# RWKV-7 in the second block's mixer: three pairs of heads through one chain of 384-column tiles

## The chip, the cores and the metric

One core of a Trainium2 chip. The metric is the device time of one execution in microseconds (us), lower is better. The kernel before takes 3003.26 us, the median of 3 runs (3002.71 to 3004.96).

## The reference, cut to what matters

The program is two transformer blocks in fp32 on 256 tokens of width 1024. The second block has two layers, each a feed-forward net, a mixer and another feed-forward net. The change is in that mixer, in its RWKV-7 part alone. It has 6 heads of 64.

```
p_a, p_b, p_c = _split(h @ w_in[l], (A_IN, B_IN, C_IN))     # layer 1 has p_mv too
r, k, v, w_lo, a_lo, g_lo = _split(shift_lerp(p_a, rwkv_mu[l]), A_SLAB)
o_a = rwkv7_mixer(r, k, v, ...)
o_b = dsa_mixer(...)          # 6 heads, 64 of up to 256 keys by an index score
o_c = retention_mixer(...)    # 4 heads
x = x + concatenate([o_a, o_b, o_c]) @ w_out[l]

# rwkv7_mixer, per head and token, S is 64x64:
sa = S @ a_t
S  = S * w_t + outer(sa, b_t) + outer(v_t, k_t)
y  = S @ r_t
y  = head_layernorm(y) * ln_w + ln_b + sum(r * k * r_k) * v
o  = y * g
```

In layer 1, v is mixed with layer 0's v first (`vfirst`).

## The kernel before, in words

`mix2` (L975) is the mixer of one layer. Its columns of `w_in` come in blocks of 128: `blk(i)` (L993) gives block i as a 128x256 product in PSUM (tag `pj`, two banks). `chunk` brings the weights of two blocks with one 1 MB DMA on SP's queue (L130), splits them into `wh` on ACT (L151) and `wl` on DVE (L152), and `mm3` (L158 to L160) makes three fp32r matmuls of every fp32 product: 24 a block, called projections here. They are the work that can fill TensorE while other work waits for other engines.

The order of the blocks in layer 0: 0 and 1 are the low-rank inputs `la` and `iwmv`; 2 to 4 are r, k, v of the first pair of heads, 5 to 7 of the second; 8 to 13 are the latent keys `ct` and the index keys and queries of the sparse attention, then its scores (L1062) and top-k (L1072, L1073); 14 to 16 are its queries `qd`, and six attention heads follow (L1092 to L1119); 17 to 19 are the third pair's r, k, v; 20 to 25 and `w_in_v` feed the retention (L1168 to L1183). Then comes `out_proj`, which needs all parts.

`rwkv` (L1187) does one pair of heads, a 128x256 tile (two heads on the partitions, 256 tokens in 4 chunks of 64). It has three parts:

- **Preparation** (L1237 to L1287), a chain of small operations on ACT, DVE, POOL and TensorE, from the square of k (L1269) to `da` and `db` (L1283).
- **Doubling** (L1301 to L1311): the inverse of a triangular 64x64 matrix per chunk and head, in 5 levels. A level is a masked copy `nm` on POOL (L1303), the product `tN·nm` (16 records on TensorE, L1209), `z` copied out by ACT (L1305), two more products, and the new `tN` and `tT` on DVE (L1308, L1310).
- **Steps** (L1324 to L1350): 4 chunks one after another. In each, `U` is copied out by ACT (L1330), the state `sn` is made on DVE (L1342) from a product and from `sd`, the old state scaled on POOL (L1341), and the output goes to `yT` (L1348). Layer norm and gate end the pair (L1352 to L1359).

Instructions are written in program order. A framework puts each on its engine's queue, by that order and by when it takes its inputs to be ready, and every engine runs its queue in a fixed order. So the place of a call decides which other work lies between its instructions. PSUM has 8 banks, by tags: `mm` 3, `pj` 2, `pr` 1, `ax` 2.

Of the kernel before, what the change touches and what calls it, by code (L numbers as in the profile page):

```python
# [73 lines left out]
class Net:  # L74
# [900 lines left out]
    def mix2(s, l, upd):  # L975
# [4 lines left out]
        with ExitStack() as cx:  # L980
# [24 lines left out]
            def lerp(p, mu, out):  # L1005
                nmu = s.small.tile([P, 1], F32, name="nmu", tag="nmu")
                V.tensor_scalar(nmu, mu, -1.0, 1.0, op0=OP.mult, op1=OP.add)
                t = k.tile([P, S + 1], F32, name="lt", tag="lt", bufs=1)
                nc.gpsimd.memset(t[:, 0:1], 0.0)
                V.tensor_tensor(t[:, 1:], p, r, OP.mult)  # L1010
                d = one("ld")
                nc.scalar.activation(d, t[:, 1:], AF.Copy, scale=nmu)
                V.scalar_tensor_tensor(out, t[:, :S], mu, d, op0=OP.mult, op1=OP.add)
                return out
# [15 lines left out]
            def rwkv(pr, b0):  # L1030
                x = [lerp(blk(b0 + i), s.col(f"mu{l}", 3 * i + pr), one("rkv", N_RKV)) for i in range(3)]
# [6 lines left out]
            V.tensor_tensor(ct, blk(8), r, OP.mult)  # L1038
            ike, iko = s.zeroed(k, 1, S, "ik")
            p = blk(9)  # L1040
# [3 lines left out]
            for b in range(4):  # L1044
                V.tensor_tensor(iq[:, b], blk(10 + b), r, OP.mult)
# [33 lines left out]
            for b in range(3):  # L1079
                V.tensor_tensor(qd[:, b], blk(14 + b), r, OP.mult)  # L1080
# [41 lines left out]

            rwkv(2, 17)
# [63 lines left out]
    def rwkv(s, l, pr, x, la, iwmv, w2, v2, cn, w, oh, ol):  # L1187
# [5 lines left out]
        rows = [slice(64 * h, 64 * h + 64) for h in range(2)]  # L1193

        def four(m):
            return m[:, None, :].to_broadcast([P, 4, 64])

        def nat(v):
            return v.rearrange("p (c t) -> p c t", c=4)

        def t1(name, bufs=1):
            return w.tile([P, S], F32, name=name, tag=name, bufs=bufs)

        def u(name):
            return nat(w.tile([P, S], F32, name=name, tag="u", bufs=N_SLOT))

        def mul(o, a, b, start=True, stop=True):
            for h, rr in enumerate(rows):
                nc.tensor.matmul(o[rr], a[rr], b[rr], start=start, stop=stop, tile_position=(64 * h, 64 * h))  # L1209

        def prod(a, b):
            p = nat(s.ax(S))
            for c in range(4):
                mul(p[:, c], a[:, c], b[:, c])
            return p

        def turn(name, x):
            p = s.ax(S).rearrange("p (g h t) -> p g h t", g=2, h=2)
            for g in range(2):
                nc.tensor.transpose(p[:, g].rearrange("p h t -> p (h t)"), x[:, 2 * g:2 * g + 2].rearrange("p c t -> p (c t)"), s.ident)  # L1220
            o = u(name)
            for c in range(2):
                for h, rr in enumerate(rows):
                    v, i = o[rr, c:4:2], p[64 * c:64 * c + 64, :, h]
                    nc.scalar.activation(v, i, AF.Copy)
            return o
# [20 lines left out]
        p = s.bank("pr", S)  # L1247
# [15 lines left out]
        dcs = s.small.tile([P, 4], F32, name="dcs", tag="dcs")  # L1263
        nc.gpsimd.tensor_copy(dcs, dd[:, 63:256:64])
# [4 lines left out]
        nc.scalar.activation(sq, kt, AF.Square, scale=s.col(f"k_k{l}", pr))  # L1269
        V.scalar_tensor_tensor(kk, kt, s.col(f"k_k{l}", pr), s.rstd(sq, 1, 2, tag="pr", floor=1e-12),  # L1270
# [3 lines left out]
        V.scalar_tensor_tensor(kt, t, 1.0, kt, op0=OP.add, op1=OP.mult)  # L1274
# [3 lines left out]
        V.scalar_tensor_tensor(t, rt, s.col(f"r_k{l}", pr), kt, op0=OP.mult, op1=OP.mult)  # L1278
        bo = t1("bo", 2)
        V.tensor_tensor(bo, s.bones(t, "pr"), vt, OP.mult)  # L1280
        nc.gpsimd.tensor_tensor(rt, rt, dd, OP.mult)
        da, db, dk, dr = u("da"), u("db"), u("dk"), nat(rt)
        V.scalar_tensor_tensor(da, nat(kk), -1.0, nat(sg), op0=OP.mult, op1=OP.mult)  # L1283
        V.tensor_tensor(db, nat(kk), nat(at), OP.mult)
        lab = u("lab")
        nc.scalar.activation(lab, prod(db, da), AF.Copy)
        nc.gpsimd.tensor_tensor(dk, nat(kt), nat(di), OP.mult)  # L1287
        vs = turn("vs", nat(vt))
        lak = u("lak")
        V.tensor_tensor(lak, prod(dk, da), four(cn("lt")), OP.mult)  # L1290
        X = u("x")
        nc.scalar.activation(X, prod(lak, vs), AF.Copy)
# [19 lines left out]
        w1 = u("w1")
        nc.scalar.activation(w1, prod(as_, tT), AF.Copy)

        mrb = u("mrb")
        V.tensor_tensor(mrb, prod(db, dr), four(cn("le")), OP.mult)
        bs = turn("bs", db)
        mrk = u("mrk")
        V.tensor_tensor(mrk, prod(dk, dr), four(cn("le")), OP.mult)
        ks = turn("ks", dk)  # L1320

        yT = t1("yT")
        st = None
        for c in range(4):  # L1324
            p = s.ax(64)
            mul(p, tT[:, c], X[:, c], stop=(c == 0))
            if c:
                mul(p, w1[:, c], st, start=False)
            U = w.tile([P, 64], F32, name="U", tag="U", bufs=2)
            nc.scalar.activation(U, p, AF.Copy)  # L1330
            if c < 3:
                p = s.ax(64)
                mul(p, ks[:, c], vs[:, c], stop=False)
                mul(p, bs[:, c], U, start=False)
                dc = dcs[:, c:c + 1]
                sn = w.tile([P, 64], F32, name="sn", tag="sn", bufs=3)
                if c == 0:
                    V.tensor_scalar(sn, p, dc, None, op0=OP.mult)
                else:
                    sd = w.tile([P, 64], F32, name="sd", tag="sd", bufs=2)  # L1340
                    nc.gpsimd.tensor_scalar(sd, st, dc, None, op0=OP.mult)  # L1341
                    V.scalar_tensor_tensor(sn, p, dc, sd, op0=OP.mult, op1=OP.add)  # L1342
            yp = s.ax(64)
            mul(yp, vs[:, c], mrk[:, c], stop=False)
            if c:
                mul(yp, st, dr[:, c], start=False, stop=False)
            mul(yp, U, mrb[:, c], start=False)
            V.tensor_copy(yT[:, 64 * c:64 * c + 64], yp)  # L1348
            if c < 3:
                st = sn  # L1350

        V.scalar_tensor_tensor(yT, s.bones(yT), -1.0 / 64, yT, op0=OP.mult, op1=OP.add)  # L1352
        sq = t1("tz1")
        nc.scalar.activation(sq, yT, AF.Square)
        V.scalar_tensor_tensor(yT, yT, s.col(f"ln_w{l}", pr), s.rstd(sq, 64, 2, tag="ax", eps=64e-5),
                               op0=OP.mult, op1=OP.mult)
        V.scalar_tensor_tensor(yT, yT, s.col(f"ln_b{l}", pr), bo, op0=OP.add, op1=OP.add)
        V.tensor_tensor(yT, yT, gt, OP.mult)
        s.split(oh, ol, yT)  # L1359
# [140 lines left out]
def host_w_in(w, mv):  # L1500
# [9 lines left out]
    bl += [P * (3 * i + pr) + r(P) for pr in range(2) for i in range(3)]  # L1510
# [3 lines left out]
    bl += [P * (3 * i + 2) + r(P) for i in range(3)]  # L1514
# [127 lines left out]
```

## Time and profile before

| | before |
|---|---|
| median of 3 runs | 3003.26 us |
| profiled execution | 3003.1 us |
| its span | 3001.1 us (2.0 us lie outside) |
| granted TensorE clock, mean | 0.996 |
| TensorE busy | 2948.9 us (98%) |
| mixer of layer 0, first projection to `out_proj` | 1991.36 to 2202.08, 210.72 us |
| mixer of layer 1 | 2577.10 to 2789.71, 212.61 us |

The page gives busy shares over the whole span, and the trace the start of every instruction. The ends of matmuls are modelled, so a row can be busy while the array waits: the distance from one start to the next says how long something really takes. An fp32 matmul that is not a projection shows as two records.

### The profile page before, as it was taken

What the parts mean: (1) busy time and instruction counts of PE and PEld (TensorE: products, weight loads), DVE (VectorE), ACT (ScalarE), POOL (GpSimd) and SP (SyncE); (2) the same over time, 40 slices, a digit from 0 to 9 for tenths busy, and PEclk for the clock granted to TensorE, in tenths of its full rate; (3) what the DMA queues carried; (4) which work ended last, traced back from release to release, by engine and by line L of the source; (5) the groups of instructions that cost most, each with busy time, mean ns of one, the idle gap of its engine ahead of it and who ended that gap; (6) DMA issues with size and microseconds to landing.
All of it is one profiled execution on the core that took longest, in us unless ns stands there. A gap on an engine that the chain in (4) does not pass through costs nothing.

```text
span 3001.1 us, 53661 instructions
## 1 busy us (share of the span) xinstructions
PE 2948.9 (98%) x21104; PEld 2590.9 (86%) x21104; DVE 2065.5 (69%) x4254; ACT 1520.6 (51%) x3106; POOL 109.7 (4%) x220
## 2 busy tenths in 40 slices
PE   8999999999999999999999999999999999999999
PEld 7888887588888888888877999998799999987998
DVE  5687766787797743335766667786677777866776
ACT  4333354754333442234666556575555655755555
POOL 0000001000000000000000000011100000111000
PEclk9999999999999999999999999999999999999999
DMA  7465422034474422322322555551245555422453
GB/s 281 159 218 194 152 99 85 15 113 169 152 262 165 151 99 92 107 82 99 122 85 99 192 174 193 197 201 54 77 145 198 188 184 190 171 75 69 169 190 127
DMA packets 86988, 434.74 MB, mean 145 GB/s; under 512 B 7888, under 2 KB 19920, under 8 KB 57296
## 3 DMA queue, kind: packets, MB, share of 16 engines
q1 hardware_dynamic: 86736, 431.31, 40.9%
q8 instruction: 166, 2.72, 0.4%
q14 instruction: 86, 0.70, 0.1%
HBM read 430.23 MB, written 1.05 MB: 144 GB/s over the span
## 4 chain that ended last, share of the span: by engine, by line
PE 78%; ACT 2%; DVE 2%; issue 1%; POOL 0%; ACTq 0%; DVEq 0%; POOLq 0%
PE mm L158 10%; PE mm L159 10%; PE mm L160 10%; PE pj L158 8%; PE pj L160 8%; PE pj L159 8%; PE pr L158 3%; PE pr L160 3%; PE pr L159 3%; PE ax L1209 3%; PE ax L562 1%; PE ax L943 1%; PE ax L741 1%; PE ax L220 0%; ACT wh L151 0%
## 5 line engine op out<-in xcount | busy, mean ns | idle before, releaser
L151 ACT ACTIVATE wh<-wr 128x512 fp32r<-128x512 f32 (+1 forms) x1341 | 824.1, 618 | 1055.4 <-PE mm L159 457.7
L152 DVE TENSOR_TENSOR wl<-wr,wh 128x512 fp32r<-128x512 f32 (+1 forms) x1341 | 897.1, 676 | 540.9 <-ACT wh L151 520.2
L158 PE MATMUL mm<-hh,wh 128*128 128x256 f32 (+1 forms) x1592 | 501.3, 315 | 0.1
L159 PE MATMUL mm<-hl,wh 128*128 128x256 f32 (+1 forms) x1592 | 500.8, 315 | 0.4 <-DVE hl L957 0.4
L160 PE MATMUL mm<-hh,wl 128*128 128x256 f32 (+1 forms) x1592 | 500.2, 314 | 0.4 <-DVE wl L152 0.4
L158 PE MATMUL pj<-hh,wh 128*128 128x256 f32 (+1 forms) x1492 | 463.5, 311 | 4.1 <-ACT hh L311 3.1
L160 PE MATMUL pj<-hh,wl 128*128 128x256 f32 (+1 forms) x1492 | 461.8, 310 | 0.2 <-DVE wl L152 0.2
L159 PE MATMUL pj<-hl,wh 128*128 128x256 f32 (+1 forms) x1492 | 459.6, 308 | 0.0
L158 PEld LDWEIGHTS mm<-hh,wh 128*128 128x128 f32 x1592 | 300.4, 189 | 20.9 <-issue 0.3
L159 PEld LDWEIGHTS mm<-hl,wh 128*128 128x128 f32 x1592 | 300.1, 188 | 21.0 <-DVE hl L957 0.8
L160 PEld LDWEIGHTS mm<-hh,wl 128*128 128x128 f32 x1592 | 299.8, 188 | 21.1 <-DVE wl L152 0.8
L254 DVE SCALAR_TENSOR_TENSOR macc<-wm,cv,macc 128x512 f32<-128x512 f32 x448 | 309.1, 744 | 0.6
L158 PEld LDWEIGHTS pj<-hh,wh 128*128 128x128 f32 x1492 | 282.2, 189 | 26.0 <-ACT hh L311 3.9
L160 PEld LDWEIGHTS pj<-hh,wl 128*128 128x128 f32 x1492 | 281.5, 189 | 16.3 <-DVE wl L152 0.4
L159 PEld LDWEIGHTS pj<-hl,wh 128*128 128x128 f32 x1492 | 281.5, 189 | 16.1 <-issue 0.9
L158 PE MATMUL mm<-ah,wh 128*128 128x256 f32 (+1 forms) x721 | 226.3, 314 | 0.0
L160 PE MATMUL mm<-ah,wl 128*128 128x256 f32 (+1 forms) x721 | 226.0, 314 | 0.0
L159 PE MATMUL mm<-al,wh 128*128 128x256 f32 (+1 forms) x721 | 226.0, 313 | 0.0
L158 PE MATMUL pr<-hh,wh 128*128 128x256 f32 (+1 forms) x518 | 166.3, 321 | 0.0
L160 PE MATMUL pr<-hh,wl 128*128 128x256 f32 (+1 forms) x518 | 165.5, 320 | 0.3 <-DVE wl L152 0.3
L159 PE MATMUL pr<-hl,wh 128*128 128x256 f32 (+1 forms) x518 | 165.8, 320 | 0.0
L158 PE MATMUL pj<-ah,wh 128*128 128x256 f32 (+1 forms) x465 | 148.6, 320 | 0.0
(589 smaller groups left out, 5054.3 us busy)
## 6 DMA issues: line engine op xcount, KB each, us to landing
wr<-f_gu SPq DMA_DIRECT2D x85, 1024.0 KB, 4.8
wr<-g_gu SPq DMA_DIRECT2D x84, 1024.0 KB, 4.8
wm<-w_mod SPq DMA_DIRECT2D x64, 1024.0 KB, 4.7
wr<-f_dn SPq DMA_DIRECT2D x64, 704.0 KB, 4.0
wr<-g_dn SPq DMA_DIRECT2D x64, 704.0 KB, 4.0
wr<-w_in_t SPq DMA_DIRECT2D x26, 1024.0 KB, 4.8
ws<-w_mod SPq DMA_DIRECT2D x8, 1024.0 KB, 9.8
wr<-ab_in SPq DMA_DIRECT2D x8, 1024.0 KB, 4.6
```

Source lines behind the costliest of these rows:

```text
L151: s.nc.scalar.activation(h, x, AF.Copy)
L152: s.nc.vector.tensor_tensor(l, x, h.bitcast(F32), OP.subtract)
L158: nc.tensor.matmul(out, lh, rh, start=start, stop=False)
L159: nc.tensor.matmul(out, lh, rl, start=False, stop=False)
L160: nc.tensor.matmul(out, ll, rh, start=False, stop=stop)
L254: nc.vector.scalar_tensor_tensor(acc[u][:, h], w[:, k, h], c, acc[u][:, h], op0=OP.mult, op1=OP.add)
L562: s.nc.tensor.transpose(p[:, b * P:(b + 1) * P], y[:, b * P:(b + 1) * P], s.ident)
L741: nc.tensor.matmul(yp[r], vA[:, k0 + kk, r], pts[e][:, kk], start=(kk == 0), stop=(kk == nk - 1), tile_position=(0, 64 * e))
L943: nc.tensor.matmul(yp[r], v[:, kk, c], pts[e][:, kk], start=(kk == 0), stop=(kk == 3), tile_position=(0, 64 * e))
L1209: nc.tensor.matmul(o[rr], a[rr], b[rr], start=start, stop=stop, tile_position=(64 * h, 64 * h))
```

## The change

- All three pairs' r, k, v come first: the host puts their nine blocks at 2 to 10, and the blocks between move up by 3.
- `rwkv_in` is called three times in a row and does the preparation of one pair. Its results go into tiles that hold all three pairs (`wide`, [128, 2, 3, 128]); its temporaries have one buffer each (so had most before). `vs` is made here, by one transpose per half.
- One call of `rwkv` does doubling and steps for all pairs: half 0 has chunks 0 and 1 of every pair, half 1 has chunks 2 and 3, each a tile of 128x384. The two halves alternate in program order, from level to level. A product is 12 small matmuls and a step handles three pairs at once.
- PSUM tiles of this chain rotate over the tags `ax`, `pr`, `ax`. The preparation uses `mm` and `pr`.
- `sd` on POOL is gone: the old state is added by a matmul with the identity (6 small matmuls in each of two steps), and one multiplication on DVE scales the sum.
- The gate's matmul moves to the end, and its copy `gt` goes; each pair has its layer norm there, ahead of `ct` and the other blocks. The third pair's call behind the heads is gone, and the retention follows the heads directly.

The diff, cut:

```
-N_SLOT = 18
+N_SLOT = 16
-            def rwkv(pr, b0):
-                x = [lerp(blk(b0 + i), ..., one("rkv", N_RKV)) for i in range(3)]
-                s.rwkv(l, pr, x, la, iwmv, w2, v2, cn, k, oh[pr], ol[pr])
-            rwkv(0, 2)
-            rwkv(1, 5)
+            wide = {n: k.tile([P, 2, 3, P], F32, name=n, tag=n) for n in ("rt", "kt", "vt", "da", "db", "vs")}
+            for pr in range(3):
+                for i, n in enumerate(("rt", "kt", "vt")):
+                    lerp(blk(2 + 3 * pr + i), s.col(f"mu{l}", 3 * i + pr), wide[n][:, :, pr])
+                s.rwkv_in(l, pr, la, iwmv, w2, v2, k, wide)
+            s.rwkv(l, la, w2, cn, k, wide, oh, ol)
...
-            rwkv(2, 17)
...
         for m in range(1, 6):
-            nm = u("nm")
-            nc.gpsimd.tensor_tensor(nm, lab, four(lv[:, m]), OP.mult)
-            z = u("z")
-            nc.scalar.activation(z, prod(nm, tN), AF.Copy)
...
+            z = [None, None]
+            for i in both:
+                nm = u("nm")
+                nc.gpsimd.tensor_tensor(nm, lab[i], units(lv[:, m]), OP.mult)
+                z[i] = u("z")
+                nc.scalar.activation(z[i], prod(nm, tN[i]), AF.Copy)
+            for i in both:
+                if m < 5:
+                    n2 = u("tN")
+                    V.tensor_tensor(n2, prod(tT[i], z[i]), tN[i], OP.add)
+                t2 = u("tT")
+                V.tensor_tensor(t2, prod(z[i], tT[i]), tT[i], OP.add)
+                tT[i], tN[i] = t2, n2
...
-                    nc.gpsimd.tensor_scalar(sd, st, dc, None, op0=OP.mult)
-                    V.scalar_tensor_tensor(sn, p, dc, sd, op0=OP.mult, op1=OP.add)
...
+                    if n:
+                        mul(p[:, r], cn("eye"), st[:, r], start=False, stop=False)
+                    mul(p[:, r], bs[i][:, r, c], U[:, r], start=False)
+                sn = state("sn", 2)
+                V.tensor_tensor(sn, p, dcs[:, :, n, None].to_broadcast([P, 3, 64]), OP.mult)
...
+        for pr in range(3):
...
+            p = s.bank("pr", S)
+            nc.tensor.matmul(p, w2[:, 2, pr * P:(pr + 1) * P], la, start=True, stop=True)
+            V.tensor_tensor(y, y, p, OP.mult)
+            s.split(oh[pr], ol[pr], y)
```

What it does to the order on TensorE, at three places of layer 0. A row is line, operation, output and operands, size, and how many in a row. `mul`'s small matmuls are L1209 before and L1289 now; projections are L158 to L160 before and L157 to L159 now. First a level of the doubling, before (the first pair, with work of the preparation of the second between):

```order
L1209 MATMUL ax<-z,tT 64x64 x8
L1209 MATMUL ax<-tT,z 64x64 x8
L1252 MATMUL pr<-la,sm 128x256
L160 MATMUL pj<-hh,wl 128x256
L1209 MATMUL ax<-tN,nm 64x64 x8
L158 MATMUL pj<-hh,wh 128x256
L159 MATMUL pj<-hl,wh 128x256
```

and now:

```order
L1289 MATMUL ax<-tN,nm 64x64 x12
L159 MATMUL pj<-hh,wl 128x256
L157 MATMUL pj<-hh,wh 128x256
L158 MATMUL pj<-hl,wh 128x256
L159 MATMUL pj<-hh,wl 128x256
L157 MATMUL pj<-hh,wh 128x256
L1289 MATMUL pr<-tN,nm 64x64 x12
L1289 MATMUL ax<-z,tT 64x64 x12
L1289 MATMUL ax<-tT,z 64x64 x12
L1289 MATMUL pr<-z,tT 64x64 x12
L1289 MATMUL ax<-tT,z 64x64 x12
L158 MATMUL pj<-hl,wh 128x256
```

A level is now six products of 12, and what stands between a product and the one that needs its result is the other half's product, and a few projections.

Second, the steps. Before (the second pair: `x·tT` and `sn·w` give U, `U·bs` and `vs·ks` the state, the others the output):

```order
L1209 MATMUL ax<-U,bs 64x64 x2
L1209 MATMUL ax<-mrk,vs 64x64 x2
L1209 MATMUL ax<-rkv,sn 64x64 x2
L1209 MATMUL ax<-mrb,U 64x64 x2
L158 MATMUL pj<-hh,wh 128x256
L159 MATMUL pj<-hl,wh 128x256
L160 MATMUL pj<-hh,wl 128x256
L158 MATMUL pj<-hh,wh 128x256
L159 MATMUL pj<-hl,wh 128x256
L1209 MATMUL ax<-x,tT 64x64 x2
```

and now (`con` is the identity):

```order
L1289 MATMUL pr<-x,tT 64x64 x2
L1289 MATMUL pr<-sn,w_20930 64x64 x2
L1289 MATMUL ax<-vs,ks 64x64 x2
L1289 MATMUL ax<-sn,con 64x64 x2
L1289 MATMUL ax<-mrk,vs 64x64 x2
L1289 MATMUL ax<-U,bs 64x64 x2
```

The projections between the steps are gone from here; there are 4 passes instead of 12, each with three times the small matmuls.

Third, the last attention head. Before, the doubling of the third pair and projections stood between its operations:

```order
L1209 MATMUL ax<-z,tT 64x64 x7
L1209 MATMUL ax<-tT,z 64x64
L1119 MATMUL mm<-lat,smd 64x256
L1209 MATMUL ax<-tT,z 64x64 x7
L159 MATMUL pj<-hl,wh 128x256
L160 MATMUL pj<-hh,wl 128x256
L1209 MATMUL ax<-tN,nm 64x64 x8
L1135 MATMUL pj<-z,con 128x256
```

and now:

```order
L159 MATMUL pj<-hh,wl 128x256
L561 MATMUL mm<-ident,pe 128x128 x3
L1117 MATMUL mm<-pt,ck 128x128 x3
L1121 MATMUL mm<-lat,smd 64x256
L1094 MATMUL mm<-qd,smd 128x256
L1103 MATMUL mm<-ct,ql 128x128
L1103 MATMUL mm<-ct,ql 128x256
L561 MATMUL mm<-ident,pe 128x128 x3
L1117 MATMUL mm<-pt,ck 128x128 x3
L1168 MATMUL mm<-qr,kre 128x256
L1121 MATMUL mm<-lat,smd 64x256
L1168 MATMUL mm<-qr,kre 128x128
```

The last head stands nearly alone, and the retention begins while it ends.

## Rows read from the trace of the kernel before

**Rows 1.** The page: busy time by engine over the span.

```profile
PE 2948.9 (98%) x21104; PEld 2590.9 (86%) x21104; DVE 2065.5 (69%) x4254; ACT 1520.6 (51%) x3106; POOL 109.7 (4%) x220
```

**Rows 2.** Windows, both mixers and a dense stretch: length, busy PE, PEld, DVE, ACT, POOL, clock, DMA.

```profile
1991.36:2202.08 210.72, 204.20 (x2313) 172.70 (x2312) 140.61 (x392) 118.52 (x296) 31.92 (x55) 1.00 0.26 89
2577.10:2789.71 212.61, 206.42 (x2320) 173.14 (x2318) 142.98 (x397) 120.33 (x299) 33.60 (x55) 1.00 0.25 88
2300.00:2310.00 10.00, 10.00 (x90) 10.00 (x89) 6.08 (x11) 4.92 (x9) 0.00 (x0) 1.00 0.81 303
```

**Rows 3.** Windows, layer 0's mixer: projections of line L158 alone, then line L1209 alone.

```profile
1991.36:2202.08 210.72, 69.66 (x235) 44.36 (x236) 1.00 0.26 89
...
1991.36:2202.08 210.72, 55.23 (x1248) 44.00 (x1248) 1.00 0.26 89
```

**Rows 4.** Timelines of TensorE, ACT and DVE: one level of the first pair's doubling.

```profile
2038.53 0.68 PE L1209 MATMUL ax<-tN,nm 64*64 64x64 f32 x16
...
2039.36 0.59 PE L972 MATMUL pr<-tmp,con 128*128 128x256 f32 x2
2039.88 0.68 PE L1209 MATMUL ax<-z,tT 64*64 64x64 f32 x16
...
2041.63 0.38 PE L1209 MATMUL ax<-tN,nm 64*64 64x64 f32 x5
...
2039.26 0.38 ACT L1305 ACTIVATE z<-ax 128x256 f32<-128x256 f32 x1 [2.01 <-PE ax L1209]
...
2040.67 0.42 DVE L1308 TENSOR_TENSOR tN<-ax,tN 128x256 f32<-128x256 f32 x1 [0.26 <-PE ax L1209]
```

**Rows 5.** Timelines of TensorE, ACT and DVE: one step of the second pair.

```profile
2092.41 0.28 PE L1209 MATMUL ax<-sn,w 64*64 64x64 f32 x4
2092.53 0.28 PE L1209 MATMUL ax<-vs,ks 64*64 64x64 f32 x4
...
2093.18 0.33 PE L1209 MATMUL ax<-U,bs 64*64 64x64 f32 x4
...
2092.74 0.22 ACT L1330 ACTIVATE U<-ax 128x64 f32<-128x64 f32 x1 [1.60 <-PE ax L1209]
...
2094.76 0.20 ACT L1330 ACTIVATE U<-ax 128x64 f32<-128x64 f32 x1
...
2093.62 0.28 DVE L1342 SCALAR_TENSOR_TENSOR sn<-ax,dcs,sd 128x64 f32<-128x64 f32 x1 [0.53 <-PE ax L1209]
```

**Rows 6.** Timelines of ACT and DVE: preparation begins and ends, layer 0 first pair, layer 1 second.

```profile
2006.62 0.51 ACT L1269 ACTIVATE tmp<-rkv,colt 128x256 f32<-128x256 f32 x1
...
2016.41 0.42 DVE L1283 SCALAR_TENSOR_TENSOR da<-kk,sgw 128x256 f32<-128x256 f32 x1
...
2614.43 0.51 ACT L1269 ACTIVATE tmp<-rkv,colt 128x256 f32<-128x256 f32 x1 [0.96 <-DVE tmp L1240]
...
2632.64 0.41 DVE L1283 SCALAR_TENSOR_TENSOR da<-kk,sgw 128x256 f32<-128x256 f32 x1
```

**Rows 7.** Groups of lines, layer 0's mixer: weight splits, masked copy, index scores, top-k; count, busy, mean.

```profile
L152 DVE TENSOR_TENSOR wl<-wr,wh 128x512 fp32r<-128x512 f32 x58 | 41.8, 726 | 7.9 <-ACT wh L151 5.8 <-PE pj L160 1.5
...
L1303 POOL TENSOR_TENSOR nm<-lab,con 128x256 f32<-128x256 f32 x15 | 12.4, 838 | 15.9 <-PE ax L1209 15.9
...
L1068 DVE SCALAR_TENSOR_TENSOR sc<-rel,iw,sc 128x128 f32<-128x128 f32 (+1 forms) x14 | 5.8, 413 | 1.0 <-ACT rel L1064 0.5
...
L1072 DVE MAX8 m<-sc 128x8 f32<-128x128 f32 (+1 forms) x16 | 5.5, 352 | 0.1
L1073 DVE MATCH_REPLACE8 sc<-m,sc 128x128 f32<-128x128 f32 (+1 forms) x16 | 5.5, 343 | 0.0
```

**Rows 8.** Windows as in Rows 2: the six heads, then the retention's last part.

```profile
2104.57:2158.37 53.80, 52.10 (x500) 42.55 (x498) 36.53 (x105) 34.19 (x100) 9.71 (x14) 1.00 0.18 60
...
2187.40:2202.08 14.68, 13.46 (x97) 10.62 (x96) 6.03 (x17) 3.82 (x8) 0.00 (x0) 1.00 0.21 71
```

**Rows 9.** The same columns, in the first block's beginning.

```profile
20.00:25.00 5.00, 3.62 (x17) 3.62 (x18) 3.90 (x9) 3.96 (x11) 0.00 (x0) 0.50 1.09 385
```

More of the change, by code (lines that the diff above doesn't have):

```diff
@@ L1012, in lerp @@
                 nc.scalar.activation(d, t[:, 1:], AF.Copy, scale=nmu)
-                V.scalar_tensor_tensor(out, t[:, :S], mu, d, op0=OP.mult, op1=OP.add)
+                like = (lambda v: v) if len(out.shape) == 2 else s.two
+                V.scalar_tensor_tensor(out, like(t[:, :S]), mu, like(d), op0=OP.mult, op1=OP.add)
                 return out
@@ L1028, in mix2 @@
             oh, ol = ([v[:, b, S:] for b in range(KT)] for v in (s.hh, s.hl))
[L1030 to L1034 removed]
+            wide = {n: k.tile([P, 2, 3, P], F32, name=n, tag=n) for n in ("rt", "kt", "vt", "da", "db", "vs")}
+            wide["dcs"] = k.tile([P, 3, 4], F32, name="dcs")
+            for pr in range(3):
[3 more added lines that the diff above has]
+            s.rwkv(l, la, w2, cn, k, wide, oh, ol)
             ct = one("ct")
[L1038 removed]
+            V.tensor_tensor(ct, blk(11), r, OP.mult)
             ike, iko = s.zeroed(k, 1, S, "ik")
[L1040 removed]
+            p = blk(12)
             V.tensor_tensor(ike[0:64, 0], p[0:64], r[0:64], OP.mult)
@@ L1185, in mix2, with two, rwkv_in @@
             s.out_proj(s.a["w_out2"][l], oh, ol, 1, upd)
-    def rwkv(s, l, pr, x, la, iwmv, w2, v2, cn, w, oh, ol):
+    def two(s, v):
+        return v.rearrange("p (a t) -> p a t", a=2)
+    def rwkv_in(s, l, pr, la, iwmv, w2, v2, w, wide):
         nc = s.nc
@@ L1192, in rwkv, with t1 @@
         E5 = math.exp(-0.5)
[L1193 to L1226, printed above, removed]
+        two = s.two
+        rt, kt, vt, da, db = (wide[n][:, :, pr] for n in ("rt", "kt", "vt", "da", "db"))
+        def t1(name):
+            return w.tile([P, S], F32, name=name, tag=name, bufs=1)
         b = slice(pr * P, (pr + 1) * P)
-        rt, kt, vt = x
         if l == 0:
-            V.tensor_copy(s.vfirst[:, pr], vt)
+            V.tensor_copy(two(s.vfirst[:, pr]), vt)
         else:
-            p = s.bank("pr", S)
+            p = s.bank("mm", S)
             nc.tensor.matmul(p, v2[:, b], iwmv, start=True, stop=True)
@@ L1237, in rwkv @@
             s.sigmoid(g, p, s.colhalf("v0", pr))
-            d = t1("tmp2")
-            V.tensor_tensor(d, s.vfirst[:, pr], vt, OP.subtract)
+            d = t1("dd")
+            V.tensor_tensor(two(d), two(s.vfirst[:, pr]), vt, OP.subtract)
             V.tensor_tensor(d, d, g, OP.mult)
-            V.tensor_tensor(vt, vt, d, OP.add)
-        p = s.bank("pr", S)
+            V.tensor_tensor(vt, vt, two(d), OP.add)
+        p = s.bank("pr", S).rearrange("p (a h t) -> p a h t", a=2, h=2)
+        for a in range(2):
+            nc.tensor.transpose(p[:, a].rearrange("p h t -> p (h t)"), vt[:, a], s.ident)
+        vs = wide["vs"].rearrange("p a r (c t) -> p a r c t", c=2)
+        for c in range(2):
+            for h in range(2):
+                nc.scalar.activation(vs[64 * h:64 * h + 64, :, pr, c], p[64 * c:64 * c + 64, :, h], AF.Copy)
+        p = s.bank("mm", S)
         nc.tensor.matmul(p, w2[:, 0, b], la, start=True, stop=True)
@@ L1273, in rwkv @@
         V.tensor_scalar(t, at, -1.0, s.col(f"k_a{l}", pr), op0=OP.add, op1=OP.mult)
-        V.scalar_tensor_tensor(kt, t, 1.0, kt, op0=OP.add, op1=OP.mult)
+        V.scalar_tensor_tensor(kt, two(t), 1.0, kt, op0=OP.add, op1=OP.mult)
         nc.gpsimd.tensor_tensor(at, at, di, OP.mult)
         t = t1("tmp")
[L1278 to L1292, printed above, removed]
@@ L1312, in rwkv @@
[L1312 to L1322, printed above, removed]
-        st = None
[L1324 to L1329, printed above, removed]
-            nc.scalar.activation(U, p, AF.Copy)
[L1331 to L1340, printed above, removed]
-                    nc.gpsimd.tensor_scalar(sd, st, dc, None, op0=OP.mult)
-                    V.scalar_tensor_tensor(sn, p, dc, sd, op0=OP.mult, op1=OP.add)
[L1343 to L1349, printed above, removed]
-                st = sn
@@ L1352, in rwkv @@
[L1352 to L1359, printed above, removed]
+        V.scalar_tensor_tensor(two(t), rt, s.col(f"r_k{l}", pr), kt, op0=OP.mult, op1=OP.mult)
@@ L1509, in host_w_in @@
     bl = [P * 9 + r(P), np.concatenate([iw, pad(24, z), 3400 + r(16), pad(80, z)])]
-    bl += [P * (3 * i + pr) + r(P) for pr in range(2) for i in range(3)]
+    bl += [P * (3 * i + pr) + r(P) for pr in range(3) for i in range(3)]
     bl += [1280 + 384 + r(P), np.concatenate([ik, ik])]
```

133 lines of the change are left out of this document (109 added, 24 removed).

## The prediction, made before the change was run

> **What bounds the kernel now.** I read the page first. TensorE is busy for 98% of the span and no other engine for more than 69% [rows 1], so a change can only give back time in which TensorE waits, and the 98% does not show it, since ends are modelled. So I went to windows. A dense stretch of projections has 90 records in 10.00 us, 0.111 us each; the mixers have 2313 records in 210.72 us and 2320 in 212.61 us [rows 2]. The mixers hold the waits, and the change touches nothing else.
>
> How much waits there is counted from prices. A projection is 0.111 us, and layer 0 has three lines of 235, so 705 [rows 2, 3]. A small matmul is two records; four records start 0.12 us after the four before them [rows 5], so 0.03 a record and about 0.058 a matmul, 1248 records in all [rows 3]. An fp32 matmul of 256 columns is two records and 0.52 us (2039.36 to 2039.88) [rows 4]; I take half, 0.26, for 128 columns, and 0.1 for those with few columns. That is 78.3 for the projections, 36.2 for the small ones, and for the other 360 records (2313 less 705 and 1248) between 0.13 and 0.26 each, mostly the smaller, some 52. Sum about 166 of 210.72. So **some 45 us a layer are waits**, and twice that is the ceiling of any gain.
>
> Where they lie: in a level of the doubling (2038.53 to 2041.63, 3.1 us) TensorE needs 3 x 16 x 0.029 = 1.4 us; the rest is z on ACT, tN on DVE and the switch to a few projections between [rows 4]. Five levels times three pairs make that 15 times. A step is 2.02 us from one U to the next, 12 steps, with sn and U between [rows 5]. The heads take 53.80 us for six, and the retention's end 14.68 us with 97 records [rows 8].
>
> **The change part by part,** for one layer, from the order of the changed program: so many instructions a stretch at the prices above. In all it has 708 projections and 636 small matmuls, so the work stays the same, and only waits can move.
>
> *Stretch A, to the last preparation* has 315 projections (35.0), 16 small matmuls (0.9), 8 of 256 columns (4.2), 8 of 128 (2.1) and 20 tiny (2.0): 44.2 us. The preparations are three in a row on temporaries with one buffer, so one waits for the one before. The nearest clean row is 9.8 us from k's square to da (2006.62 to 2016.41) [rows 6]; three new blocks are 72 x 0.111 = 8.0 us plus some 2.8 of its own matmuls, 10.8. So a preparation hides behind the next pair's projections if it stays below that. I add 4 us for start and end: **48**, between 45 and 56 (the latter with preparations of 14 us).
>
> *Stretch B, the chain* has 620 small matmuls (36.0), 89 projections (9.9), 24 transposes (6.2) and one more (0.5): 52.6. A level has 6 products of 12, each 0.7 us, 4.2 us. One half alone would need its three products one after another, 2.1, plus z (ACT: 0.22 at 64 columns, 0.38 at 256 [rows 4, 5], so 0.49 at 384 as an estimate), tN and tT on DVE (0.28 and 0.42 give 0.51 each) and some 0.4 of handing over: 3.5 to 4.0, less than the 4.2 of both. So the halves cover one another. Masked copies on POOL, 0.84 mean at 256 columns [rows 7], so up to 1.26, are not in that path: they need `lab` alone, and two are 2.5 a level. In the steps the projections are gone; a step is about 2.6 us of small matmuls, but TensorE waits for U, which ACT needs 0.3 for after the product, and partly for sn: 0.5 us a step. The eye matmuls are 12 x 0.058 = 0.7, in the 36.0. With 2 for the steps, 2 at the levels, 3 until the first tN (lab, mask, add, transpose, four copies in a row): **59.6**, between 53 and 68.
>
> *Stretch C, layer norms, scores, top-k* has 171 projections (19.0), 19 of 256 columns (9.9), 15 of 128 (3.9) and 20 tiny (2.0): 34.8. Covered by DVE's work: top-k 2 x 5.5, scores 5.8 [rows 7], three layer norms at about 3.5, splits of 7 blocks at 0.726 for some 8 (58 for 26 chunks), blocks and the index parts some 4: 37. The two engines are level; I take **38**, between 34 and 43. The price of putting pairs ahead is here: top-k now has no chain beside it, but no third pair behind it either.
>
> *Stretch D, heads and retention* has 133 projections (14.8), 15 of 256 columns (7.8), 45 of 128 (11.7), 6 of 64x256 (3.1) and 24 tiny (2.4): 39.8. The heads' pace before is 53.80 us with a preparation and a doubling between them [rows 8]; without the third pair they are freer, but the last head's own chain (scores, softmax, transposes, output) stands with 6 projections only: **44**, between 40 and 48. The retention's last part is bare as before, at 14.68 [rows 8]; its first scores now stand within the last head: **12.5**, between 11 and 16.
>
> Here a rule speaks against the change. The clock was granted at 1.00 (2.4 GHz) through the retention's bare 14.68 us [rows 8], so I cost the longer bare tail at the high level. The Trainium skill, page "TensorE: Matmul & The Clock Gate", section "HAM oscillation — how this bites in real kernels", says that short bursts of matmuls with waits between can send the array back to the low clock each time; by that the tail would cost some 12 us more and the sum come out at 3010 (rival 4).
>
> **Sum:** 48 + 59.6 + 38 + 44 + 12.5 = 202.1 against 210.72, -8.6 in layer 0. Layer 1 begins 1.9 us higher [rows 2]; its extra for v (one matmul, five small operations a pair) stands in the preparations, which take over a part of the waits of before, so I take -8.5 there. Together -17.1, from the profiled execution's 3003.1 (which is 0.16 below the median of the runs): **2986.0 us**. SP's queue has the same 26 weight loads a layer, in one run of nine blocks more, and POOL loses sd and keeps the masked copies: no term of either.
>
> **The rivals.**
> 1. *Cover is nearly complete.* The halves leave no gap, and the top-k runs beside projections. A 45, B 55, C 36, D 54.5: 190.5, -20.2 a layer, **2963 us**. For it: 45 us of waits stand there to be had [rows 2, 3]. Against: 89 projections are few for 59 us of chain.
> 2. *No net change.* C is bound by DVE at 43 and the retention, without a doubling's matmuls to fill, is at 16: 48 + 60 + 43 + 44 + 16 = 211, **3003 us**. For it: DVE's 37 us in C lack every wait. Against: 171 projections there.
> 3. *Slower, by the preparations.* They run three in a row with one buffer for each temporary, and DVE splits weights at the same time. Layer 1's second took 18.2 us (2614.43 to 2632.64) [rows 6]. A pair period of more than 10.8 goes straight to the time, since the chain needs all three. At 15 the gain is used up (3 x 4.2, less the 4 that stands in A); at 15.5 to 18, as in that row, it is 3 x 5.9 less 4 = +13.7 less 8.6, some 5 a layer: **3013 us**. Against: that row had another pair's mrb and mrk ahead of it on DVE, and the first pair's 9.8 had not.
> 4. *The clock falls in the tail.* In 20 to 25 us it was granted at 0.50 (1.2 GHz), where TensorE was busy for 3.62 of 5 us [rows 9]; through the bare 14.68 us before `out_proj` it stayed at 1.00 [rows 8], so I hold little of it. The work of the last 12 to 14 us would take twice as long, some 12 a layer, from -8.6 to about +3.5: **3010 us**.
> 5. *It doesn't do what it says:* the order shows the 12s and both halves alternating. The time would stay at 3003.
>
> **How the numbers follow.** A measurement of this kernel can tell about 0.2% from no change, 6 us. Chances: the forecast 0.58, with its own range of 2968 to 3000; complete cover 0.14; no net change 0.12; preparations 0.11; clock 0.03; not done 0.02. The forecast's range comes from the bounds: lows together give 183 a layer and highs 231, but they do not fall together; half of the way to the lows gives 9 more a layer (2968), and 7 of the 29 to the highs use up what is gained but for 3 us (3000). The range reaches to the middle of the first rival's lows and over the no-change case: 2960 to 3008; outside stay the last two slower cases and a part of the first rival. Faster by over 0.2%: 0.52 of the forecast's 0.58, and 0.14: 0.66. Same: 0.06, 0.12 and 0.02: 0.20. Slower: 0.11 and 0.03: 0.14.
>
> **What would show it.** The mixer of layer 0 at about 202 us. From the first projection to the last da about 48, with preparations of about 10 us; from there to the last yT about 60, a level of both halves at 4.2 to 4.8 us; heads at under 8 us each; the stretch from the last head's output to `out_proj` at 12 to 13. It is wrong if preparations are over 14 us (rival 3), if TensorE's clock is below 1.00 in the tail (rival 4), or if a level takes over 6 us because the three banks of the chain let the halves wait for each other, which I have put into the 68 only.

## The result, and the profile after

The changed kernel takes **3025.24 us** (median of 4 runs, 3024.59 to 3026.5) against 3003.7 (4 runs): a ratio of 1.0072, 95% interval 1.0055 to 1.0089. It is slower by 21.5 us where 17 us less was forecast, and lies outside the range. Its profiled execution took 3026.5, with a span of 3024.7 and a mean granted TensorE clock of 0.989 (0.996 before).

First the page of the changed kernel, busy time by engine [rows 1], and windows of both mixers (length; busy PE, PEld, DVE, ACT, POOL; clock; DMA) [rows 2]:

```profile
PE 2950.9 (98%) x21152; PEld 2607.6 (86%) x21152; DVE 2053.1 (68%) x4194; ACT 1502.2 (50%) x3036; POOL 102.0 (3%) x202
```

```profile
1995.89:2214.68 218.79, 199.81 (x2337) 174.05 (x2336) 133.14 (x362) 110.07 (x262) 27.60 (x46) 0.95 0.25 86
2597.38:2807.91 210.53, 195.69 (x2344) 171.84 (x2342) 136.44 (x367) 109.10 (x263) 30.24 (x46) 0.98 0.25 89
```

The page says nothing; the windows say two things. The mixers are 218.79 and 210.53 us, together 6.0 more than before. And layer 0's begins at 1995.89, 4.5 us later than before, although nothing ahead of it was edited. Of the 23.6 us between the spans, 17.6 lie **outside the mixers**, nearly all in the four feed-forward nets of the second block: layer 0's first takes 177.9 us before and 182.2 after. Windows of 60 us in that net, before, then after:

```profile
1900.00:1960.00 60.00, 60.00 (x532) 60.00 (x531) 45.71 (x85) 34.99 (x64) 0.00 (x0) 1.00 0.53 185
```

```profile
1903.00:1963.00 60.00, 60.00 (x512) 60.00 (x512) 44.14 (x82) 33.57 (x62) 0.00 (x0) 1.00 0.49 175
```

532 projections became 512: 113 ns each became 117 (118 from start to start), at the same granted clock and with TensorE never idle.

The mixers by the forecast's stretches (ends: third da, last yT, first transposes of a head behind the top-k, last head's output, `out_proj`):

| us | A | B | C | heads | retention | sum |
|---|---|---|---|---|---|---|
| forecast | 48 | 59.6 | 38 | 44 | 12.5 | 202.1 |
| layer 0 | 50.8 | 61.5 | 43.8 | 43.3 | 19.5 | 218.8 |
| layer 1 | 55.0 | 61.9 | 34.2 | 39.9 | 19.6 | 210.5 |

Five views of the changed kernel show what stands in them. Windows in B's doubling, in C, at the last head and in the retention; DVE's writes of `tT` for the first half in two levels of the doubling; TensorE's longest idle time in C; DVE's timeline behind the last head; the retention's table `dec`, its readers and its load:

```profile
2063.00:2069.00 6.00, 6.00 (x156) 5.61 (x155) 2.92 (x5) 1.50 (x4) 1.96 (x3) 1.00 0.02 7
...
2135.00:2141.00 6.00, 3.16 (x17) 3.11 (x18) 6.00 (x22) 2.73 (x5) 0.74 (x1) 0.83 0.38 156
2183.00:2195.00 12.00, 8.67 (x26) 5.10 (x26) 2.16 (x7) 3.16 (x12) 0.00 (x0) 0.52 0.01 1
2195.23:2214.68 19.45, 13.97 (x70) 10.16 (x69) 5.06 (x15) 3.37 (x7) 0.00 (x0) 0.78 0.09 27
```

```profile
2059.74 0.56 DVE L1339 TENSOR_TENSOR tT<-ax,tT 128x384 f32<-128x384 f32 x1
...
2065.80 0.56 DVE L1339 TENSOR_TENSOR tT<-ax,tT 128x384 f32<-128x384 f32 x1
```

```profile
2137.84 0.70 PE L1135 MATMUL pj<-z,con 128*128 128x256 f32 x2 [2.90 <-DVE z L1133]
```

```profile
2199.45 0.62 DVE L1171 TENSOR_TENSOR st<-mm,dec 128x256 f32<-128x256 f32 x2 [2.71 <-DMA dec<-con]
```

```profile
L1171 DVE TENSOR_TENSOR st<-mm,dec x16: 280/358/425, 2199.5 to 2804.6; 128x256 f32<-128x256 f32 x8, 128x128 f32<-128x128 f32 x8
L1160 SPq DMA_DIRECT2D dec<-con x2: 328/328/328, 2195.9 to 2788.7; - x2
...
  DMA dec<-con: 5.4, 2
```

The doubling runs dense, a level in 6.06 us. In C, DVE is busy for 6.00 of 6.00 us (top-k, and between it weight splits and the reading of blocks out of `pj`) and TensorE for 3.16: its longest idle time, 2.90 us, ends with such a reading, `z`. Around the last head TensorE's clock is granted at 0.52. And DVE waits 2.71 us a layer for a load that is issued at 2195.9, when the last head is done. Before, the same row of `dec` reads:

```profile
L1160 SPq DMA_DIRECT2D dec<-con x2: 328/328/328, 2159.0 to 2751.0; - x2
```

### The profile page after: what moved, and what is told of

It reads as the page before. It is cut to its first block, busy times and chain, and to the rows that moved or that the text cites. A ratio compares the mean times of both kernels' runs of the same rounds, so it can differ in the third digit from the quotient of the medians.

```text
span 3024.7 us, 53549 instructions
## 1 busy us (share of the span) xinstructions
PE 2950.9 (98%) x21152; PEld 2607.6 (86%) x21152; DVE 2053.1 (68%) x4194; ACT 1502.2 (50%) x3036; POOL 102.0 (3%) x202
## 3 DMA queue, kind: packets, MB, share of 16 engines
q1 hardware_dynamic: 86736, 431.31, 40.5%
## 4 chain that ended last, share of the span: by engine, by line
PE 76%; DVE 3%; ACT 2%; issue 1%; DMA 0%; POOL 0%; ACTq 0%; DVEq 0%; POOLq 0%
PE mm L157 10%; PE mm L158 10%; PE mm L159 10%; PE pj L157 8%; PE pj L158 8%; PE pj L159 8%; PE pr L157 3%; PE pr L159 3%; PE pr L158 3%; PE ax L1289 2%; PE ax L561 1%; DVE wl L151 1%; PE pr L1289 1%; PE ax L942 1%; PE ax L740 1%
## 5 line engine op out<-in xcount | busy, mean ns | idle before, releaser
L157 PE MATMUL mm<-hh,wh 128*128 128x256 f32 (+1 forms) x1592 | 503.7, 316 | 0.2
L158 PE MATMUL mm<-hl,wh 128*128 128x256 f32 (+1 forms) x1592 | 503.0, 316 | 0.7 <-DVE hl L956 0.7
L159 PE MATMUL mm<-hh,wl 128*128 128x256 f32 (+1 forms) x1592 | 502.4, 316 | 0.4 <-DVE wl L151 0.4
L157 PE MATMUL pj<-hh,wh 128*128 128x256 f32 (+1 forms) x1492 | 464.8, 312 | 4.2 <-ACT hh L310 3.1
L158 PE MATMUL pj<-hl,wh 128*128 128x256 f32 (+1 forms) x1492 | 460.1, 308 | 0.1
L159 PE MATMUL pj<-hh,wl 128*128 128x256 f32 (+1 forms) x1492 | 459.6, 308 | 0.2 <-DVE wl L151 0.2
L159 PEld LDWEIGHTS mm<-hh,wl 128*128 128x128 f32 x1592 | 302.0, 190 | 21.2 <-DVE wl L151 0.8
L157 PEld LDWEIGHTS mm<-hh,wh 128*128 128x128 f32 x1592 | 301.1, 189 | 21.2 <-ACT hh L955 0.6
L158 PEld LDWEIGHTS mm<-hl,wh 128*128 128x128 f32 x1592 | 300.8, 189 | 21.3 <-DVE hl L956 1.1
L157 PEld LDWEIGHTS pj<-hh,wh 128*128 128x128 f32 x1492 | 283.1, 190 | 24.5 <-ACT hh L310 3.9
L159 PEld LDWEIGHTS pj<-hh,wl 128*128 128x128 f32 x1492 | 283.3, 190 | 15.1 <-issue 0.8
L158 PEld LDWEIGHTS pj<-hl,wh 128*128 128x128 f32 x1492 | 282.7, 189 | 15.5 <-issue 0.7
L157 PE MATMUL mm<-ah,wh 128*128 128x256 f32 (+1 forms) x721 | 227.1, 315 | 0.0
L159 PE MATMUL mm<-ah,wl 128*128 128x256 f32 (+1 forms) x721 | 226.8, 315 | 0.0
L158 PE MATMUL mm<-al,wh 128*128 128x256 f32 (+1 forms) x721 | 226.7, 314 | 0.0
L157 PE MATMUL pr<-hh,wh 128*128 128x256 f32 (+1 forms) x518 | 166.8, 322 | 0.0
L159 PE MATMUL pr<-hh,wl 128*128 128x256 f32 (+1 forms) x518 | 166.0, 320 | 0.3 <-DVE wl L151 0.3
L158 PE MATMUL pr<-hl,wh 128*128 128x256 f32 (+1 forms) x518 | 166.3, 321 | 0.0
L157 PE MATMUL pj<-ah,wh 128*128 128x256 f32 (+1 forms) x465 | 149.0, 321 | 0.0
```

Of the source, the lines that this page charges most:

```text
L157: nc.tensor.matmul(out, lh, rh, start=start, stop=False)
L158: nc.tensor.matmul(out, lh, rl, start=False, stop=False)
L159: nc.tensor.matmul(out, ll, rh, start=False, stop=stop)
```

## Experiments

All are compared with runs of the kernel before on the same chip (median 3002.68 to 3003.5). The experiments ran on three chips: e1 to e4, e5 to e8, and e9 to e12; between these the median of the kernel before differs by 0.8 us.

### The loss outside the mixers: the place in SBUF (e1, e2, e7)

`dcs` was a tile of the pool `small`, four buffers of 32 bytes a partition. The change put it elsewhere, so all tiles behind that pool, the nets' `ah` and `al` among them, moved down by 128 bytes: in the built programs `ah` begins at 0 bytes beyond a multiple of 512 before, and at 384 after. (SBUF is where these tiles lie. `ah` and `al` are the two parts into which a net's inner activations are split, as `hh` and `hl` are of its input.) e1 puts 128 unused bytes back into the changed kernel; e2 moves `dcs` in the kernel before.

```
# e1, in mix2                                     # e2, in before's rwkv
+ s.small.tile([P, 4], F32, name="dcp", ...)      - dcs = s.small.tile([P, 4], F32, ...)
                                                  + dcs = w.tile([P, 4], F32, ..., bufs=4)
```

> The changed kernel with 128 bytes per partition put back into the pool from which dcs was taken, and nothing else. Theory (place): the mixers explain only 6.0 us of the loss (218.8 + 210.5 against 210.7 + 212.6); 17.6 us lie outside them, in the four feed-forward nets of the second block, where 1024 projections each that read ah and al come every 118 ns instead of every 113, because these tiles moved down by 128 bytes in SBUF. Then this gives 3025.2 - 17.6 = about 3008, and the projections stand at 113 again. Rival (the chip): the 118 ns are a state of the chip or of TensorE's queue in these executions, or come from what the mixer left behind; then it stays at about 3025.

> The kernel before with one edit: dcs lies in the mixer's pool, as in the changed kernel, so that the feed-forward nets' tiles move down by the same 128 bytes. Place: about 17.6 us slower than before, 3021, with 118 ns for ah and al. Rival: 3003, as before.

e1: 3010.99 us, ratio to before 1.0028 (1.0018 to 1.0039); its profiled execution, 3006.0, is the fastest of eight. Its mixers are 216.24 and 211.00 us, so 2577.0 of its span lie outside them, as before (2577.8). e2: 3019.12, ratio 1.0054 (1.0037 to 1.0071), 16.4 us slower. The same 60 us in e1, and in e2:

```profile
1903.00:1963.00 60.00, 60.00 (x532) 60.00 (x531) 46.82 (x88) 35.62 (x66) 0.00 (x0) 1.00 0.52 181
```

```profile
1900.00:1960.00 60.00, 60.00 (x512) 60.00 (x511) 43.66 (x81) 33.85 (x61) 0.00 (x0) 1.00 0.51 178
```

The bytes take the slow spacing with them both ways, and the whole net, 178.0 us in e1 and 182.2 in e2. The place it is; the rival falls.

e7 is e1 with the four nets at four places, `ah` at 64 and 128 (layer 0) and 192 and 256 (layer 1) beyond a multiple of 512:

```
- s.ffn(a["g_gu"][l], ..., s.upd2(0.5), 128, True)
+ s.ffn(a["g_gu"][l], ..., s.upd2(0.5), 128 + (64, 192)[l], True)
- s.ffn(a["g_gu"][2 + l], ..., s.upd2(0.5), 128, True)
+ s.ffn(a["g_gu"][2 + l], ..., s.upd2(0.5), 128 + (128, 256)[l], True)
```

> As e1, with the four feed-forward nets of the second block at four other places in SBUF: ah and al begin 64, 128, 192 and 256 bytes beyond a multiple of 512. e1 has them at 0 with 113 ns a projection, the changed kernel at 384 with 118. If the place within 512 bytes decides, in relation to the weights (64 beyond a multiple), the four nets show different spacings, each constant through the net, 113 or 118 or more; if only an alignment to 512 is good, all four show 118 and the time is about 3029; if it was something else that went with the 128 bytes, all show 113 and the time is 3011.

One execution: 3014.97. Windows with the first 30 us that read `ah`, then the projections of `hh` behind them at 64 bytes; then a net at 128 and one at 256:

```profile
1873.00:1903.00 30.00, 30.00 (x253) 30.00 (x252) 17.77 (x32) 13.63 (x24) 0.00 (x0) 1.00 0.58 203
1905.00:1960.00 55.00, 55.00 (x488) 55.00 (x487) 42.65 (x80) 32.40 (x61) 0.00 (x0) 1.00 0.51 183
...
2291.00:2409.00 118.00, 118.00 (x1003) 118.00 (x1002) 85.60 (x162) 67.39 (x125) 0.00 (x0) 1.00 0.56 195
...
2883.00:2972.00 89.00, 89.00 (x786) 89.00 (x785) 64.83 (x121) 49.57 (x90) 0.00 (x0) 1.00 0.54 190
```

That is 119 and 113 ns at 64 bytes (192 does the same), 118 throughout at 128, 113 throughout at 256. So 0 and 256 are good, 128 and 384 bad, 64 and 192 bad only while `ah` is read. The place decides, as first expected, but the spacing is not constant through a net, as that expectation had it, and a plain rule of multiples of 512 fails too.

Nor is 0 good without exception. In the kernel before, with `ah` at 0 in all four nets, the last 256 projections of layer 0's first net come every 113 ns and those of its second every 117 (windows in each):

```profile
1963.00:1990.00 27.00, 27.00 (x239) 27.00 (x238) 22.64 (x45) 18.69 (x38) 0.00 (x0) 1.00 0.66 224
2370.00:2399.00 29.00, 29.00 (x249) 29.00 (x248) 23.60 (x46) 19.26 (x39) 0.00 (x0) 1.00 0.61 210
```

So something besides the place enters; no run isolates it.

### The retention: its table's load (e9, e10)

`dec` uses the buffer `iq`, which holds the heads' weights `smd` until the last head. e9 (on e1) and e10 (on e5, below) give it four tiles of the chain's ring, free since the steps' end.

```
- dec = k.tile([P, 4 * S], F32, name="dec", tag="iq")
...
+ decs = [k.tile([P, 384], F32, name="dec", tag="u", bufs=N_SLOT) for h in range(4)]
```

> As e1, with the retention's decay table in four tiles of the chain's ring (free once the chain ends) instead of the buffer that the heads' weights hold until the last head is done. In e1 the table's load is issued at 2186.7 us, behind the last head, and DVE waits for it 2.7 us a layer (5.5 in both); before the change it was issued at 2159.0, 14 us ahead of its use. Theory (this load is a wait that the third pair had covered): from the last head's output to the output projection 17 us instead of 19 to 20.5, and 5 to 7 us in all: 3004 to 3006. Rival (something else is late next, the banks mm or the low clock): less than 2 us.

> As e5, with the same table moved. In e5 the tail is filled with projections of the output projection, so the wait for the table is partly covered: between 0 and 5 us below e5's 2970.4; if the whole wait stood on the path even there, 5 to 7.

e9: 3000.21, 10.8 below e1 (12.3 below e11, which is level with e1 and ran on e9's chip) and level with before (ratio 0.999, 0.9979 to 1.0001). From the last head's output to `out_proj`, in e1 and then in e9:

```profile
2186.08:2206.50 20.42, 15.16 (x71) 11.06 (x69) 5.06 (x15) 3.37 (x7) 0.00 (x0) 0.67 0.08 26
2774.56:2793.80 19.24, 13.46 (x71) 9.75 (x69) 5.05 (x15) 3.38 (x7) 0.00 (x0) 0.82 0.09 27
```

```profile
2188.15:2202.40 14.25, 11.31 (x70) 8.31 (x68) 4.50 (x15) 3.38 (x7) 0.00 (x0) 0.91 0.00 0
2769.71:2784.50 14.79, 11.86 (x70) 8.75 (x68) 4.69 (x15) 3.38 (x7) 0.00 (x0) 0.88 0.00 0
```

Together 10.6 us less with the same work: the wait of 5.5, and then more than the wait. Times (1 - clock) the first pair has lost 10.2 us of clock, the second 3.1; that 7 us is room enough for the rest, though nothing here isolates it. e10: 2972.82, no gain on e5's 2970.44; in e5's trace DVE no longer waits for the load.

### C: the top-k beside the chain (e3)

On e1: index blocks and scores are written ahead of `s.rwkv(...)`, the top-k loop behind it, in place in the bias tiles.

```
-            s.rwkv(l, la, w2, cn, k, wide, oh, ol)
             ct = one("ct")
...
-                sc = tmp("sc", "gi")[:, :nk]
+                sc = k.tile([P, nk], F32, name=f"bi{t}")
...
+            s.rwkv(l, la, w2, cn, k, wide, oh, ol)
+            for t in range(2):
...
+                V.tensor_scalar(sc, sc, TAKEN, FAR, op0=OP.not_equal, op1=OP.mult)
```

> As e1, and the index blocks and scores are written ahead of the chain, the top-k behind it, so that DVE's top-k fills gaps of the chain. Theory (the stretch between chain and heads is bound by DVE: the first head waits until 2153 for the top-k, 45 us behind the chain's end where 38 was forecast): the heads begin 8 to 15 us sooner relative to the chain's end, and 6 to 12 us a layer come back, so 2984 to 2996 if e1 is 3008. Rival (that wait is covered by projections anyway): within 5 us of e1, since the projections used up there are missing in the tail.

2991.15, ratio 0.9965 (0.9952 to 0.9978): 19.8 below e1. Layer 0's top-k now ends amid the chain (DVE's timeline), and the first head's transposes begin at 2121.92, ahead of the chain's last product at 2123.04 (TensorE's):

```profile
2083.19 0.41 DVE L1078 MATCH_REPLACE8 bi<-m,bi 128x256 f32<-128x256 f32 x1
```

```profile
2121.92 0.44 PE L561 MATMUL mm<-ident,pe 128*128 128x128 f32 x2
...
2123.04 0.28 PE L1290 MATMUL ax<-mrb,U 64*64 64x64 f32 x4
```

In the changed kernel C, 43.8 us, lay between them. The work of C (projections, norms) now stands elsewhere; what went is the stretch in which TensorE waited for DVE. In the profiled executions most of the gain is layer 0's: its mixer is 13.6 us shorter than e1's, layer 1's 3.2.

### The bare tail and its clock (e4, e6, e8)

e4 (on e1) and e8 (on the kernel before) let `out_proj` use banks that are free at the time:

```
-            ps = [s.mm(T) for j in range(2)]
+            tags = (("ax", "ax"), ("pj", "pj"), ("mm", "pr"), ("mm", "mm"))[c]
+            ps = [s.bank(tags[j], T) if units == 1 else s.mm(T) for j in range(2)]
```

> As e1, and the output projection of the second block takes its first two column pairs in the banks ax and pj, which are free at that time, so that 72 projections a layer that need only the first six blocks can stand between the last heads and the retention. Theory (the tail is bare and TensorE waits there, and its clock is granted at 0.50 to 0.8 while it does): 8.1 us of projections a layer go into waits, and the clock stays at 1.00, worth some 5 to 8 more: 2980 to 2990 if e1 is 3008. Rival (the clock is not what costs, the tail is bound by its own chain over ACT and DVE): the 8.1 us alone, so about 2992. Second rival (they are drawn up so early that the tail is as bare as before): within 4 us of e1.

> The kernel before with the edit of e4 alone (output projection's first columns in the banks ax and pj). If the bare tail is the same cost before as after the change, it gains what e4 gained over e1, 18 us: 2985. If the tail is a cost that the change has made (the third pair's doubling covered it before), it gains no more than the 14.7 us of the retention's end filled with 8 us of projections, 2 to 8 us a layer: 2987 to 2999.

e4: 2993.0, 18 below e1. Its mixers are as long as e1's (215.47 and 212.75 against 216.24 and 211.00 us) but hold 71 more records each, 142 x 0.113 = 16.0 us: nearest the first rival, the 8.1 us a layer alone. Part of what these cover is the wait for the table's load, 5.5 us in e1 and 0.2 here. e8: 3000.58, ratio 0.9992 (0.9982 to 1.0001), no difference. There the framework moved only some 16 records a layer into the mixer, so it does not test the tail of before as meant.

e6 (on e1) adds 24 matmuls a layer that take the last head's `lat` and whose results nobody reads; its work is larger by them:

```
+            for i in range(12):
+                p = s.ax(S)
+                for j in range(2):
+                    nc.tensor.matmul(p, lat[:, :P], lat, start=(j == 0), stop=(j == 1))
             s.out_proj(s.a["w_out2"][l], oh, ol, 1, upd)
```

> As e1, with 24 matmuls a layer of 256 columns that nobody reads, behind the last head's latent output, so that TensorE is busy through the retention's tail. About 11 us of work a layer is added and none is moved. Theory (the low clock in the tail costs time): the clock is granted at 1.00 there and the tail from the last head's output to the output projection falls from 20 us to 15 to 17, the whole 3 to 10 us below e1, 3001 to 3008. Rival (the tail is bound by ACT and DVE alone): the tail stays at 20, the whole within 3 us of e1. Second rival (the added work stands in the way): 5 to 20 us above e1.

3011.85, level with e1. The tail in e6:

```profile
2190.61:2211.50 20.89, 20.89 (x114) 15.33 (x112) 4.87 (x15) 3.38 (x7) 0.00 (x0) 0.96 0.09 26
2778.32:2798.40 20.08, 20.08 (x113) 14.86 (x111) 4.87 (x15) 3.38 (x7) 0.00 (x0) 1.00 0.09 27
```

The clock came back and the tail stayed at 20. With the table's load in it, TensorE's pace was not what bound the tail, or the added work (43 records at some 0.26 us, 11 us) took back what the clock gave; e6 cannot tell these apart.

### All together, and the preparations' buffers (e5, e11, e12)

e5 has the edits of e1, e3 and e4. In e11 (on e1) and e12 (on e10) the second pair's temporaries lie in another lane:

```
         def t1(name):
+            if pr == 1:
+                return w.tile([P, S], F32, name=name, tag="gi", bufs=LANES["gi"])
```

> The edits of e3 (scores ahead of the chain, top-k beside it) and e4 (72 projections of the output projection free for the tail) together, with the 128 bytes. If they mend two separate waits, the gains add: 3011 - 20 - 18 = about 2973. If both only bring the same projections into the same bare tail, about 2988, no more than the better one.

> As e1, with the second pair's temporaries of the preparation in buffers of the heads' lane, so that it need not wait for the first pair's, nor the third for the second's. Forecast's third rival in small (preparations wait for one another's buffers): from the first to the third da it was 25.9 us in layer 0 and 28.8 in layer 1 of e1 where 21.6 was forecast (2 x 10.8); with two sets it falls to 22 to 23, and the whole by 6 to 10 us: 3001 to 3005. Rival (the preparations are paced by ACT, DVE and the projections, not by buffers): da to da stays within 1 us and the whole within 3 us of e1.

> As e10, with the temporaries of e11. If both theories hold, e10 less 6 to 10 us: 2958 to 2962; if only the table's, e10.

**e5: 2970.44 us**, ratio 0.9893 (0.9877 to 0.991): the gains of e3 and e4 add (40.5 below e1), and it beats both kernels by 1.1% and 1.8%. Its tail:

```profile
2173.84:2192.80 18.96, 18.92 (x142) 15.98 (x140) 8.05 (x20) 6.20 (x12) 0.00 (x0) 1.00 0.41 139
```

142 records instead of 71, at 1.00. In both of its mixers the clock stays at 1.00, where e1's have 0.96 and 0.98, some 13 us of clock; how much of the 40.5 that is, no run separates. e11: 3012.54, level with e1, and from first to third da 25.7 us in layer 0 against 25.9, 31.6 in layer 1 against 28.8. e12: 2971.8, as e10. So in layer 0 the preparations do not wait for one another's buffers. In layer 1 the new lane made them longer, against both expectations, and the third pair still takes the first's buffers, so e11 does not decide it there.

## Why the prediction was wrong

The profiled execution is 40.5 us over the forecast: 17.6 outside the mixers, 16.7 in layer 0's (218.8 against 202.1) and 6.4 in layer 1's (210.5 against 204.1).

**The largest part, by a step that was not a term at all:** "the change touches nothing else" than the mixers. The edit took one small tile out of a pool, and the nets behind it moved. The move back gave 14.3 us (e1 against after), the same move in the kernel before cost 16.4 (e2), and 17.6 lie outside the mixers in the profiles. Without it the change would have been 8 us slower than before (e1), not 21.5; so the place alone did not turn the direction, and the terms below did the rest. The whole diff shows the move, `dcs` leaving `s.small`; the prediction does not speak of it.

**The retention, 12.5 forecast, 19.5 and 19.6 measured.** "Bare as before, at 14.68" [rows 8] took a row in which the table had long been there. What the third pair's place covers was asked for TensorE's waits and not for the load that stood behind the heads' weights. Nor was that stretch bare: 35 of its 97 records are projections, and 6 of the 70 now. With the load moved (e9) the stretch is 14.25 and 14.79, about the old length with less work in it, and still 2 us over the forecast.

**Stretch C, 38 forecast, 43.8 and 34.2 measured.** DVE's sum of 37 was near, and rival 2's 43 was layer 0's outcome; layer 1's is shorter because 123 projections stand in it and not the 171 that I counted (19 more stand in A, 32 more in the heads). The error was to see projections as cover: their weights pass DVE, and their results leave `pj` by DVE, and while DVE does the top-k, TensorE has 17 records in 6 us. e3 shows its price, 19.8 us in both layers, where the forecast's C had 3 us of waits in each.

**A and B, 48 and 59.6, were low by 3 to 7 and by 2.** The halves alternate as the order said and cover one another: in a level no two of TensorE's starts lie more than 0.22 us apart. That a level takes 6.06 us, not the 4.2 to 4.8 given as a sign, is no wait of the halves, and the sign "over 6 us" came true without its cause: its six products take 4.5 us (0.70 to 0.84 each) and ten projections between them 1.6, which stand in B's sum but were left out of the sign. The steps, 3.1 us from one yT to the next, were right. From one da to the next it is 13.9 and 12.1 us in layer 0 and 15.0 and 13.9 in layer 1, not 10.8. So rival 3's price came in part, but in layer 0 not by its mechanism (single buffers), as e11 shows; what paces the preparations stays open. Layer 1's A is long by 19 more projections, some 2.1 us, and by the extra matmuls on v, which I had counted as covered.

**Heads:** 44 forecast, 43.3 measured in layer 0, right; 39.9 in layer 1, just under the lower bound. Layer 0's figure is partly luck: the clock of 0.52 around the last head stands in it, which I had not counted.

**Rival 4, the clock, held at 0.03, did occur.** It was granted 0.52 around the last head and 0.78 in the retention where I expected 1.00; clock lost in the two mixers, length times (1 - clock), comes to 0.05 x 218.79 + 0.02 x 210.53 = 15 us, an estimate from rounded clocks of about the most that it can have cost. The Trainium skill, "TensorE: Matmul & The Clock Gate", "HAM oscillation — how this bites in real kernels", says that matmuls in bursts with waits between them fall back to the low clock. This trace agrees: 26 records in the 12 us at 0.52. My reason against it was one stretch at 1.00 [rows 8] that had dense work just ahead and projections in it; here the head ahead of it was bare too. How much of the loss is the clock's own stays open: e6 found none, e9's ten executions suggest much (below).

In short: the mechanism forecast for the chain works. With the place and the top-k put right the same chain gives 2991 (e3), and 2970 when `out_proj` fills the tail as well (e5), which is an edit beyond the forecast's change. What was wrong is what the move uncovered.

## What to carry to other kernels

When a diff moves a tile from one pool to another, compare the addresses of everything behind it, and look at the spacing of dense matmuls far from the edit. When a block of work is moved away, list the loads that landed while it ran, by the buffer each waits for, and ask what covers them now. Work that passes an engine (weights split on DVE, results read there) is no cover for a wait on that engine.

## What the runs showed of the hardware

The spacing of an fp32r matmul of 256 columns had two values, 113 and some 118 to 119 ns, at a granted clock of 1.00 throughout, and which of them went, with the exception shown at e7, with the place where its operand begins within 512 bytes (0 and 256 fast, 128 and 384 slow). At 128 and 384 the projections of `hh`, which had not moved, were slow too when they followed those of `ah`; at 64 and 192 they were not. Why is open.

Executions of one and the same program differed with the mean granted clock: e9's ten reach from 2994.59 us (0.993) to 3009.04 (0.988), some 3 us for 0.001, which is 0.001 of the span. Whether the clock makes the time or longer waits lower the clock, these do not show. The kernel before stayed at 0.994 to 0.996 and within 6 us.

In C of the changed kernel, a few projections behind the idle 2.90 us, the granted clock falls to 0.50. Projections then come every 0.21 us, where they come every 0.113 at 1.00:

```profile
2139.00:2142.30 3.30, 3.30 (x18) 3.30 (x17) 2.43 (x8) 0.63 (x1) 0.36 (x1) 0.50 0.00 0
```

Whether the kernel's time carries those 1.6 us is not shown, since DVE is busy there too.
